# Layer two's memory attention first, sample steps per pair of heads, six state updates after the gates: a two-layer hybrid decoder step on one Trainium2 core

## The chip, the core and the metric

The kernel runs on one core of a Trainium2 chip. The metric is device time in microseconds: the median of the runs, and beside it one profiled execution with the busy times of the engines. PE is TensorE (its matmuls; PEld are its weight loads), DVE is VectorE, ACT is ScalarE, POOL is GpSimd, and SP issues the large transfers. A projection is a product of a 2048 x 128 block of weights with the activations of 264 tokens.

## What is computed

One step of a trunk of two layers for 256 prompt tokens and 8 sample tokens that share the weights. Layer one is sliding-window attention. Layer two, where the change lies, is an HGRN2 recurrence with 12 heads. Both have four memory cross-attention heads, a SiLU gate, an output projection and a LayerNorm. For layer two the reference says, shortened:

```
q, f, iv, mq, g = _split(h @ w_in, HG_SPLITS)
fg = lb + (1 - lb) * sigmoid(f);  qh = silu(q);  kh = 1 - fg;  gh = log(fg)
# per token t, head h:  state = fg * state + kh (x) v ;  o = qh . state
o = o * rsqrt(mean(o*o) + eps) * norm_w                  # per head
mem_o = softmax(mq . mk / sqrt(128)) . mv                # 4 memory heads
branch = concat(o, mem_o) * silu(g);  y = branch @ w_out
h = LN(alpha * h + y)
```

For the prompt the recurrence starts from zero and runs in chunks; its last state is an output. For each of the 8 samples the 12 states (128 x 128 numbers each) are read, used for one token, updated and written back, and the memory keys and values come from a cache.

## The kernel before

**The stream.** All weights and caches come as units of 128 x 2048 f32 numbers (1 MB), in an order written out in the code (`stream.add`). `Stream.load` (L79) has SP fetch a unit into one of four raw slots. `Stream.prep` splits it into two f16 halves: ACT writes the high half (L97), DVE the low half (L98). At most four units are split ahead. `Stream.run` then calls the unit's function. A projection (`proj`) is 16 blocks with three matmuls each (high x high, high x low, low x high, L303 to L305). A raw slot is free for the next load once its unit is split, except for a state unit, whose raw numbers are updated in place and written out.

**Side work.** After each unit, `after` calls `pump(1)`, which runs one step of the generator at the head of the queue `side`: a pair's chunked recurrence (`hg_side`, ten steps) or one memory head's prompt attention (`memp_side`, two steps). The lists `later` and `due` put off short pieces by one unit.

**The planner.** The code gives a program order, dependences and a few fixed orders (`issue_after`, `keep_in_program_order`). A planner sets the order of each engine's instructions and gives out the slots of the tile pools when the program is built, from priorities that follow the program order and from its own estimates of durations.

**Layer two.** Heads go in pairs. Per pair come two forget-gate units (`f_unit`), two value units (`hv_unit`), and per head a query unit (`hq_unit`), a state unit of half size (`state_unit`) and, for heads 0 to 7 (`NG1`), that head's gate (`early_gate`, stored unmultiplied in `mix`). The query unit of the odd head appends the pair's `hg_side`. A state unit forms the sample token's output: eight samples, each one matmul of two columns and one of one column against the state's halves (L1222, L1223), two all-ones matmuls for q.k (L1226), and small DVE and ACT operations on 8 numbers per partition (L1212 to L1229). Then it updates the state: eight selection matmuls spread the value rows (`vb`, L1233), ACT scales the state by the forget gate (L1237), DVE adds k times v (L1238), and POOL stores it to `ss_o` (L1241). `f_unit` makes `ks8`, the scaled k, for this (L1003).

After the sixth pair come the four memory queries (`mq_unit`); the last of them appends the four `memp_side`. Then four units of cached keys (`ck_unit`, small matmuls into `mss`; after the fourth a softmax with two transposes back, `mback`, L677), and four of cached values (`cv_unit`, `mso`), with the gates 8 to 15 (`gate_unit`) between and behind them. A gate from 8 on is multiplied in by `gate_fin` once its head is done.

The output projection has 16 units (`out_unit`). The last eight are done for 176 of the 264 tokens first and keep their halves (`hold`, a pool that opens when layer two's pool has been closed); the other 88 tokens follow while the first 176 are normalised.

Of the kernel before, what the change touches and what calls it, by code (L numbers as in the profile page):

```python
# [18 lines left out]
P = 128  # L19
NC = 16  # L20
# [13 lines left out]
NG1 = 8  # L34
# [12 lines left out]
LEVELS = (1, 2, 4, 8, 16, 32, 64)  # L47
NMASK = (len(LEVELS) - 1) * 64

# [8 lines left out]
class Stream:  # L58


    def __init__(self, nc, pool, nraw, nsplit):
        self.nc, self.pool = nc, pool
        self.nraw, self.nsplit = nraw, nsplit
        self.units = []
        self.raw = {}
        self.hl = {}

# [37 lines left out]
    def run(self, pump):  # L105
# [11 lines left out]
        for i in range(n):  # L117
# [8 lines left out]
            while free < prepped and (free <= i or self.units[free][5]):  # L126
                free += 1
# [7 lines left out]
def trunk_kernel(  # L135
# [75 lines left out]
    bias_s = pm.tile([P, 2, NQ], F32, name="bias_s")  # L211

# [770 lines left out]
    def f_unit(h):  # L983
        def fn(hl):
# [6 lines left out]
            if i == 0:  # L991
# [3 lines left out]
                cur["ks8"] = p1.tile([P, 2, TS], F32, tag="ks8", name=f"ks8{h}", bufs=2)  # L995
            fg, kk, ks8 = cur["fg"][:, i], cur["kk"][:, i], cur["ks8"][:, i]
# [6 lines left out]
            nc.vector.tensor_scalar_mul(ks8, kk, 1.0 / (SA * SK))  # L1003
# [5 lines left out]
    def hq_unit(h):  # L1009
        def fn(hl):  # L1010
            p1 = H["p"]
            pt = proj(hl, xhl, T, f"hq{h}")
            if h % 2 == 0:
                cur["q"] = p1.tile([P, 2, T], F32, tag="hq", name=f"hqs{h}", bufs=2)
            silu2(cur["q"][:, h % 2], pt)
            if h % 2 == 1:
                side.append(hg_side(h // 2, cur["q"], cur["vn"], cur["fg"], cur["qk"]))
# [3 lines left out]
    later, due = [], []  # L1021

    def hv_unit(h):
        def fn(hl):
# [3 lines left out]
            if i == 0:  # L1028
                cur["vn"] = p1.tile([P, 2, 2, P], F32, tag="vn", name=f"vn{h}", bufs=2)
                cur["vr"] = p1.tile([P, 2, P], F16, tag="vr", name=f"vr{h}", bufs=2)  # L1030
# [10 lines left out]
    def hv_rows(h, vt, vs, vn, vr):  # L1041
# [7 lines left out]
        nc.vector.tensor_copy(vr[:, i], p16)  # L1049
# [14 lines left out]
    def hg_side(pi, q, vn, fg, qk):  # L1064
# [119 lines left out]
        for i, sq in enumerate(sqs):  # L1184
# [3 lines left out]
            scaled = mix[:, h] if h >= NG1 else sq  # L1188
# [3 lines left out]
            if h < NG1:  # L1192
# [4 lines left out]
    def state_unit(h):  # L1197
        def fn(hl):
            p1 = H["p"]
            pi, i = h // 2, h % 2  # L1200
            raw = stream.raw[state_at[h]][:, : TS * P]
            R = raw.rearrange("p (b v) -> p b v", b=TS)
            v = hl[:, :, : TS * P].rearrange("p s (b v) -> p s b v", b=TS)
            vr, fgs, ks8 = cur["vr"][:, i], cur["fg"][:, i, TP:T], cur["ks8"][:, i]
            qs, vts = (cur[n][:, i, TP:T] for n in ("q", "vt"))
            ks = cur["kk"][:, i]
            if i == 0:
                osb[pi] = p1.tile([P, 2, T], F32, tag="osb", name=f"osb{pi}", bufs=2)
            qk = p1.tile([P, TS], F32, tag="qk", name=f"qk{h}", bufs=2)
            qf = p1.tile([P, TS], F32, tag="qf", name=f"qf{h}", bufs=2)  # L1210
            qfh = p1.tile([P, TS, 2], F16, tag="qfh", name=f"qfh{h}", bufs=2)
            nc.vector.scalar_tensor_tensor(qf, qs, SA * 0.5 * CP, fgs, op0=ALU.mult, op1=ALU.mult)  # L1212
            nc.vector.scalar_tensor_tensor(qk, qs, 8.0 * 0.5 * CP / SK, ks, op0=ALU.mult, op1=ALU.mult)
            qkh = p1.tile([P, 2, TS], F16, tag="qkh", name=f"qkh{h}", bufs=2)
            nc.scalar.activation(qkh[:, 0], qk, AF.Copy)
            nc.vector.tensor_tensor(qkh[:, 1], qk, qkh[:, 0], op=ALU.subtract)
            nc.scalar.activation(qfh[:, :, 0], qf, AF.Copy)
            nc.vector.tensor_tensor(qfh[:, :, 1], qf, qfh[:, :, 0], op=ALU.subtract)
            po = bank("ms", 1, f"hos{h}")
            pov = po[:, : 2 * TS].rearrange("p (b s) -> p b s", s=2)  # L1220
            for b in range(TS):
                mm(pov[:, b], v[:, 0, b], qfh[:, b], start=True, stop=False)  # L1222
                mm(pov[:, b, 0:1], v[:, 1, b], qfh[:, b, 0:1], start=False, stop=True)  # L1223
            pq = po[:, 2 * TS : 3 * TS]
            for s in range(2):
                mm(pq, H["ones"], qkh[:, s], start=s == 0, stop=s == 1)  # L1226
            nc.vector.tensor_reduce(qf, pov, axis=AX.X, op=ALU.add)
            nc.vector.tensor_tensor(qk, pq, vts, op=ALU.mult)
            nc.vector.scalar_tensor_tensor(osb[pi][:, i, TP:T], qf, 1.0 / (SA * SA), qk, op0=ALU.mult, op1=ALU.add)  # L1229
            for g in range(2):  # L1230
                pvb = bank("pt", 2, f"vb{h}{g}")
                for bb in range(4):
                    mm(pvb[:, bb * P : (bb + 1) * P], H["sel"][:, 4 * g + bb], vr, start=True, stop=True)  # L1233
                for bb in range(4):
                    b = 4 * g + bb
                    s = R[:, b]
                    nc.scalar.activation(s, s, AF.Copy, scale=fgs[:, b : b + 1])  # L1237
                    nc.vector.scalar_tensor_tensor(  # L1238
                        s, pvb[:, bb * P : (bb + 1) * P], ks8[:, b : b + 1], s, op0=ALU.mult, op1=ALU.add
                    )  # L1240
            nc.gpsimd.dma_start(ss_o[pi, :, i * TS * P : (i + 1) * TS * P], raw)  # L1241
# [3 lines left out]
    state_at = {}  # L1245
    for pi in range(HD // 2):
        for part, unit in (("f", f_unit), ("v", hv_unit)):
            for i in range(2):
                stream.add(wb(w_in1, NB1[part] + 2 * pi + i), unit(2 * pi + i))
        for h in (2 * pi, 2 * pi + 1):  # L1250
            stream.add(wb(w_in1, NB1["q"] + h), hq_unit(h))
            state_at[h] = len(stream.units)
# [180 lines left out]
```

## Time and profile before

| | us |
|---|---|
| median of 3 runs (lowest, highest) | 906.13 (906.07, 907.13) |
| profiled execution | 906.08 |
| its span, first to last instruction | 904.3 |
| PE busy, share of the span | 886.6 (98%) |
| DVE busy | 701.5 (78%) |
| ACT busy | 582.4 (64%) |
| POOL busy | 34.9 (4%) |

Times in the trace count from the first instruction. In this execution layer two's first projection starts at 420 us, the memory queries at 702, the first cache unit at 729 and the output projection at 800. "Idle before" a row is the time in which its engine stood still, and the name behind the arrow is what ended it. Matmuls overlap, so a matmul's own duration is longer than the step from one start to the next; the step is what a matmul costs.

### The profile page before, as it was taken

Reading aid. Unit: us, or ns where it says so; the run is one execution under the profiler, and the core shown is the slowest. Engines: PE = TensorE matmul, PEld = TensorE weight load, DVE = VectorE, ACT = ScalarE, POOL = GpSimd, SP = SyncE. Lnnn points to the kernel's source line nnn. Section 1 sums busy time; section 2 is a strip of 40 time slices with the busy share of each in tenths; the row PEclk is TensorE's granted clock in tenths of the full one; section 3 lists DMA queues with packets and bytes.
Section 4 is the critical chain, followed back from the end, with each engine's and each line's share of the span. In section 5 each row is a group of like instructions: output and inputs, shape, how many; then the busy total and the mean of one; then the engine's idle time right before and its main releaser. Section 6 shows DMA issues by size and latency. Waiting matters only on the chain.

```text
span 904.3 us, 21814 instructions
## 1 busy us (share of the span) xinstructions
PE 886.6 (98%) x9281; PEld 762.9 (84%) x9281; DVE 701.5 (78%) x1230; ACT 582.4 (64%) x982; POOL 34.9 (4%) x68
## 2 busy tenths in 40 slices
PE   9999999999999999999999999999999999799996
PEld 6888889678888888876888888898888888688996
DVE  6879877669886666697687887979788989678736
ACT  6767776657664444476766877777777585858415
POOL 1100010000000000002000000000000000000000
PEclk9999999999999999999999999999999999899999
DMA  9998566557785555556374655827454878456303
GB/s 340 392 353 317 188 245 209 188 208 265 262 333 192 187 192 203 207 198 214 127 292 137 216 201 174 299 101 260 160 215 164 303 283 308 172 207 244 130 2 97
DMA packets 37853, 198.67 MB, mean 220 GB/s; under 512 B 4555, under 2 KB 10732, under 8 KB 17532
## 3 DMA queue, kind: packets, MB, share of 16 engines
q1 hardware_dynamic: 33024, 181.55, 56.3%
q0 software_dynamic: 4688, 15.67, 4.6%
q8 instruction: 72, 1.18, 0.5%
q14 instruction: 25, 0.20, 0.1%
q10 hardware_dynamic: 44, 0.07, 0.0%
HBM read 180.03 MB, written 17.22 MB: 218 GB/s over the span
## 4 chain that ended last, share of the span: by engine, by line
PE 77%; DVE 8%; ACT 6%; DMA 6%; issue 3%; SPq 0%; ACTq 0%; DVEq 0%
PE o L303 5%; PE o L305 5%; PE o L304 5%; PE g L305 5%; PE g L303 5%; PE g L304 5%; DVE hl L98 4%; ACT hl L97 2%; PE hv L305 2%; PE hv L303 2%; PE hv L304 2%; DMA raw<-in_w_in 2%; PE hq L303 2%; PE hq L305 2%; PE hq L304 2%
## 5 line engine op out<-in xcount | busy, mean ns | idle before, releaser
L98 DVE SCALAR_TENSOR_TENSOR hl<-raw,hl 128x2048 f16<-128x2048 f32 (+2 forms) x168 | 358.6, 2138 | 82.0 <-ACT hl L97 81.0
L97 ACT ACTIVATE hl<-raw 128x2048 f16<-128x2048 f32 (+2 forms) x168 | 299.2, 1784 | 97.8 <-PE o L305 45.4
L305 PEld LDWEIGHTS <-hl 128*128 128x128 f16 (+2 forms) x2048 | 197.4, 98 | 31.8 <-DVE hl L98 2.9
L303 PEld LDWEIGHTS <-hl 128*128 128x128 f16 (+2 forms) x2048 | 197.3, 98 | 30.6 <-issue 2.2
L304 PEld LDWEIGHTS <-hl 128*128 128x128 f16 (+2 forms) x2048 | 197.4, 98 | 30.3 <-issue 2.2
L305 PE MATMUL g<-xhl,hl 128*128 128x264 f16 x512 | 142.0, 277 | 2.4 <-DVE hl L98 2.4
L303 PE MATMUL g<-xhl,hl 128*128 128x264 f16 x512 | 141.9, 277 | 0.0
L304 PE MATMUL g<-xhl,hl 128*128 128x264 f16 x512 | 141.9, 277 | 0.0
L303 PE MATMUL o<-mix,hl 128*128 128x264 f16 x384 | 105.4, 276 | 0.8 <-DVE xres L747 0.8
L304 PE MATMUL o<-mix,hl 128*128 128x264 f16 x384 | 105.8, 276 | 0.0
L305 PE MATMUL o<-mix,hl 128*128 128x264 f16 x384 | 105.7, 276 | 0.0
L303 PE MATMUL q<-xhl,hl 128*128 128x264 f16 x192 | 53.0, 276 | 1.0 <-DVE kst L251 1.0
L303 PE MATMUL f<-xhl,hl 128*128 128x264 f16 x192 | 52.9, 276 | 0.4 <-DVE mvhl L251 0.4
L305 PE MATMUL hv<-xhl,hl 128*128 128x264 f16 x192 | 53.0, 276 | 0.0
L303 PE MATMUL hq<-xhl,hl 128*128 128x264 f16 x192 | 53.0, 276 | 0.0
L304 PE MATMUL hq<-xhl,hl 128*128 128x264 f16 x192 | 53.0, 276 | 0.0
L305 PE MATMUL hq<-xhl,hl 128*128 128x264 f16 x192 | 53.0, 276 | 0.0
L304 PE MATMUL hv<-xhl,hl 128*128 128x264 f16 x192 | 53.0, 276 | 0.0
L303 PE MATMUL hv<-xhl,hl 128*128 128x264 f16 x192 | 53.0, 276 | 0.0
L304 PE MATMUL q<-xhl,hl 128*128 128x264 f16 x192 | 53.0, 276 | 0.0
L305 PE MATMUL q<-xhl,hl 128*128 128x264 f16 x192 | 53.0, 276 | 0.0
L304 PE MATMUL f<-xhl,hl 128*128 128x264 f16 x192 | 52.9, 276 | 0.0
(338 smaller groups left out, 1858.4 us busy)
## 6 DMA issues: line engine op xcount, KB each, us to landing
raw<-in_w_in SPq DMA_DIRECT2D x88, 1024.0 KB, 6.4
raw<-in_w_o SPq DMA_DIRECT2D x32, 1024.0 KB, 5.0
raw<-in_w_mk SPq DMA_DIRECT2D x8, 1024.0 KB, 4.9
raw<-in_w_mv SPq DMA_DIRECT2D x8, 1024.0 KB, 4.9
raw<-in_c_mk SPq DMA_DIRECT2D x8, 1024.0 KB, 5.1
raw<-in_c_mv SPq DMA_DIRECT2D x8, 1024.0 KB, 7.0
raw<-in_state SPq DMA_DIRECT2D x12, 512.0 KB, 5.4
out_ss<-raw POOLq DMA_DIRECT2D x12, 512.0 KB, 5.5
```

The source lines that it names most:

```text
L97: hi = self.nc.scalar.activation(hl[:, 0, s], raw[:, s], AF.Copy, scale=scale)
L98: lo = self.nc.vector.scalar_tensor_tensor(hl[:, 1, s], raw[:, s], scale, hl[:, 0, s], op0=ALU.mult, op1=ALU.subtract)
L303: mm(out, lhs(0), rhs(0), start=start, stop=False)
L304: mm(out, lhs(0), rhs(1), start=False, stop=False)
L305: return mm(out, lhs(1), rhs(0), start=False, stop=stop)
```

## The change

Layer two's units get another order, one state unit per pair takes the place of two, and six heads' state updates move into the output projection.

- **Order.** `f 0`, the four memory queries, the four key-cache and four value-cache units stand among the units of pairs 0 and 1; state units are dealt out by hand. `EARLY` gates are those of heads 0, 1, 2 and 6; the other twelve gates follow the last pair, with 10 and 11 last.
- **Pumps.** `pumps` says for each unit how many side steps run after it (0, 1 or 2 in place of 1).
- **State per pair.** One 1 MB unit for two heads: the small operations work on 16 numbers, the all-ones matmuls on 16 columns, so there are 12 in place of 24. `sel` carries the scale that `ks8` had. For pairs 0 to 2 head `2 pi` is updated at once and the other one unit later (`later`), and `stream.longer` keeps the raw slot one unit longer in the program order.
- **Put off.** For heads 6 to 11 (`LATER`) the forget gates and keys are copied behind the value rows and stored to DRAM (`kept`). At the seventh of the twelve gates POOL fetches `sel`, the kept rows and the first three states again, the states into the memory heads' tiles `mkhl`, `mvhl` and `mqhl`, which are free by then. Output units 1, 3, 5, 7, 9 and 11 each update one head and fetch the state that is three further on into the home just used.

```
-NG1 = 8
+EARLY = (0, 1, 2, 6)
+LATER = tuple(range(6, HD))
...
-            while free < prepped and (free <= i or self.units[free][5]):
+            while free < prepped and (free + self.longer.get(free, 0) <= i or self.units[free][5]):
...
-            nc.vector.tensor_scalar_mul(ks8, kk, 1.0 / (SA * SK))
...
-                cur["vr"] = p1.tile([P, 2, P], F16, tag="vr", name=f"vr{h}", bufs=2)
+                cur["vr"] = p1.tile([P, 2, KEPT], F32, tag="vr", name=f"vr{h}", bufs=2)
...
+    def update(h, R, vr, fgs, ks, sel):
+        for g in range(2):
+            pvb = bank("pt", 2, f"vb{h}{g}")
+            for bb in range(4):
+                mm(pvb[:, bb * P : (bb + 1) * P], sel[:, 4 * g + bb], vr, start=True, stop=True)
+            for bb in range(4):
+                b = 4 * g + bb
+                s = R[:, b]
+                nc.scalar.activation(s, s, AF.Copy, scale=fgs[:, b : b + 1])
+                nc.vector.scalar_tensor_tensor(
+                    s, pvb[:, bb * P : (bb + 1) * P], ks[:, b : b + 1], s, op0=ALU.mult, op1=ALU.add
+                )
+        nc.gpsimd.dma_start(ss_o[h // 2, :, h % 2 * TS * P : (h % 2 + 1) * TS * P], R.rearrange("p b v -> p (b v)"))
+
+    def fetch(h):
+        if not homes:
+            aside["sel"] = cp.tile([P, TS, P], F16, tag="ms", name="late_sel", bufs=2)
+            nc.gpsimd.dma_start(aside["sel"], sel_d)
+            aside["kept"] = cp.tile([P, len(LATER), KEPT], F32, tag="ms", name="late_kept", bufs=2)
+            for pi in sorted(kept):
+                k = 2 * pi - LATER[0]
+                nc.gpsimd.dma_start(aside["kept"][:, k : k + 2], kept[pi])
+            for t in (mkhl, mvhl, mqhl):
...
+        homes.rotate(-1)
+        aside[h] = homes[-1]
+        nc.gpsimd.dma_start(aside[h], state[h // 2][:, (h % 2) * TS * P : (h % 2 + 1) * TS * P])
...
+    def with_update(fn, k):
+        def f(hl):
+            fn(hl)
+            late_update(LATER[k])
+            if k + 3 < len(LATER):
+                fetch(LATER[k + 3])
...
+            split_from(qfh[:, :, :, 0], qfh[:, :, :, 1], qf, 1.0)
+            split_from(qkh[:, 0], qkh[:, 1], qk, 1.0)
...
+                mm(pq, H["ones"], qkh[:, s].rearrange("p i b -> p (i b)"), start=s == 0, stop=s == 1)
...
+            if 2 * pi in LATER:
+                tail = vr[:, :, P // 2 :]
+                nc.vector.tensor_copy(tail[:, :, :TS], fgs)
+                nc.vector.tensor_copy(tail[:, :, TS:], ks)
+                nc.gpsimd.dma_start(kept[pi], vr)
+                return
...
+            half(0)
+            later.append(lambda: half(1))
...
+    f_of(0)
+    for h in range(NM):
+        w1("mq", h, mem1_sides(mq_unit(h)) if h == NM - 1 else mq_unit(h))
+    cache(c_mk, ck_unit, 0)
+    f_of(1, 2)
+    cache(c_mk, ck_unit, 1)
+    v_of(0, 2)
+    cache(c_mk, ck_unit, 2)
+    v_of(1)
+    cache(c_mk, ck_unit, 3)
+    q_of(0)
+    gate_of(0)
+    cache(c_mv, cv_unit, 0)
+    gate_of(1)
+    cache(c_mv, cv_unit, 1)
+    q_of(1)
+    cache(c_mv, cv_unit, 2)
+    f_of(2, 2)
+    cache(c_mv, cv_unit, 3)
+    f_of(3, 2)
+    state_of(0)
+    v_of(2, 2)
+    v_of(3, 2)
+    q_of(2)
+    q_of(3)
+    state_of(1)
+    gate_of(2)
+    for pi in range(2, HD // 2):
+        gated = 2 * pi - 2 in EARLY
+        f_of(2 * pi, 2)
+        f_of(2 * pi + 1, 2)
+        v_of(2 * pi, 2)
+        v_of(2 * pi + 1, 1 if gated else 2)
+        q_of(2 * pi)
+        q_of(2 * pi + 1)
+        state_of(pi)
+        if 2 * pi in EARLY:
+            gate_of(2 * pi)
...
+    for k, j in enumerate([j for j in range(NC) if j not in EARLY and j not in last] + list(last)):
+        w1("g", j, fetch_first(gate_unit(1, j)) if k == 6 else gate_unit(1, j))
     for i in range(NC):
-        stream.add(wb(w_o[1], i), out_unit(1, i), home=hold if i >= NC - NSPLIT else None)
+        unit = out_unit(1, i)
+        if i % 2 == 1 and i // 2 < len(LATER):
+            unit = with_update(unit, i // 2)
+        stream.add(wb(w_o[1], i), unit, home=hold if i >= NC - NSPLIT else None)
...
-        pump(1)
+        pump(pumps.get(i, 1))
...
-        sel[b, b] = 1
-        sel[TS + b, b] = 1
+        sel[b, b] = 1 / (SA * SK)
+        sel[TS + b, b] = 1 / (SA * SK)
```

139 lines of the change are left out of this document (70 added, 69 removed).

## The prediction

> **What bounds the kernel now.** I read the page first, then who waited for whom on PE, then the busy times by stretch, then single rows where PE stood still.
>
> ```profile
> span 904.3 us, 21814 instructions
> ...
> PE 886.6 (98%) x9281; PEld 762.9 (84%) x9281; DVE 701.5 (78%) x1230; ACT 582.4 (64%) x982; POOL 34.9 (4%) x68
> ...
> PEclk9999999999999999999999999999999999899999
> ```
>
> PE is busy in 886.6 of 904.3 us, so an edit pays by matmuls it takes out or by moments in which PE stands still or runs at a lower clock. The granted clock dips in one slice, the 35th of 40, near 780 us. The waits of PE, layer two up to 736 us (first row) and 736 to 806 us (the rest), say the same:
>
> ```profile
> PE f L303 <- DVE mvhl L251: 0.4, 1, 0.4
> ...
> PE g L305 <- DVE hl L98: 2.4, 2, 1.7
> PE hpo L1169 <- ACT st L1147: 1.5, 1, 1.5
> PE mback L677 <- DVE mrows L674: 1.0, 1, 1.0
> PE msc L303 <- ACT osq L1183: 0.4, 1, 0.4
> PE hpo L1171 <- ACT s L1162: 0.3, 1, 0.3
> ```
>
> In 317 us of recurrences PE waits 0.4 us; in the 70 us behind them, where the memory attention, the last two recurrences and the late gates meet, 2.4 + 1.5 + 1.0 + 0.4 + 0.3 = **5.6 us**. The stretches (span, then busy time of PE, PEld, DVE, ACT, POOL, then granted clock, DMA share, GB/s) show why:
>
> ```profile
> 419.00:455.00 36.00, 35.57 (x334) 30.75 (x332) 21.46 (x46) 25.27 (x49) 6.16 (x11) 1.00 0.49 171
> ...
> 508.00:561.00 53.00, 52.85 (x565) 46.71 (x564) 45.12 (x89) 39.02 (x70) 2.14 (x4) 1.00 0.61 211
> ...
> 736.00:765.00 29.00, 28.37 (x363) 24.94 (x361) 28.97 (x33) 19.94 (x21) 0.00 (x0) 1.00 0.89 328
> 765.00:785.00 20.00, 15.56 (x231) 12.93 (x229) 12.74 (x22) 13.88 (x22) 0.54 (x1) 0.91 0.45 165
> ...
> 806.00:848.00 42.00, 41.23 (x371) 35.63 (x370) 33.73 (x37) 28.73 (x28) 0.00 (x0) 1.00 0.60 223
> 848.00:876.00 28.00, 28.00 (x372) 28.00 (x370) 11.10 (x27) 2.87 (x8) 0.00 (x0) 1.00 0.01 2
> ```
>
> The first stretch (heads 0 and 1 before any recurrence runs) leaves DVE 14.5 of 36 us free. A full pair, 508 to 561, has DVE 45.1 in 53 (85%) and PE does not wait. From 736 to 765 DVE is busy in 28.97 of 29 us: there a PE-cheap cache unit follows nearly every gate. Then the split weights run out and PE loses 4.4 of 20 us. These rows show how cheap a cache unit is for PE:
>
> ```profile
> 777.00 0.17 PE L696 MATMUL mso<-msphl,hl 128*128 128x2 f16 x1
> ...
> 777.25 0.16 PE L696 MATMUL mso<-msphl,hl 128*128 128x2 f16 x1
> ...
> 788.78 0.28 PE L304 MATMUL g<-xhl,hl 128*128 128x264 f16 x1
> ...
> 789.68 0.28 PE L303 MATMUL g<-xhl,hl 128*128 128x264 f16 x1
> ```
>
> Ten steps in 0.25 us make 25 ns, and 32 of them 0.8 us a cache unit; eight steps in 0.90 us make 112.5 ns, and 48 of them 5.4 us a projection. DVE and ACT split the same megabyte for either:
>
> ```profile
> L98 DVE SCALAR_TENSOR_TENSOR hl<-raw,hl 128x2048 f16<-128x2048 f32 x69 | 158.0, 2292 | 23.9 <-ACT hl L97 23.4
> L1238 DVE SCALAR_TENSOR_TENSOR raw<-vb,ks,raw 128x128 f32<-128x128 f32 x96 | 26.7, 345 | 0.2 <-PE vb L1233 0.2
> L98 DVE SCALAR_TENSOR_TENSOR hl<-raw,hl 128x1024 f16<-128x1024 f32 x12 | 14.7, 1222 | 1.8 <-ACT hl L97 1.7
> L734 DVE SCALAR_TENSOR_TENSOR sil<-sil,g 128x264 f32<-128x264 f32 x8 | 3.4, 428 | 0.0
> ...
> L1237 ACT ACTIVATE raw<-raw,fg 128x128 f32<-128x128 f32 x96 | 29.5, 391 | 3.5 <-DVE hl L98 3.5
> L1226 PE MATMUL hos<-qkh,ones 128*128 128x8 f16 x24 | 2.3, 166 | 0.0
> ```
>
> **The change, part by part.** *Removed from the end of layer two:* the eight cache units, the four memory queries and the memory heads' prompt work. Twelve gates remain there with the last recurrence: PE 12 x 5.4 = 64.8, and about 7.5 of the 9.8 us that the pair row leaves beside its eight projections (53 - 43.2), 72 us in all. DVE: 12 splits, 27.5; the pair's own work, 45.1 less its splits (8 x 2.29 + 2 x 1.22 = 20.8) and updates (16 of 96, 4.5), 19.8, which includes two gates; three operations of 0.43 for each of the other ten, 12.9. That is 60 of 72 us, 84%, the share of the pair row, under which PE did not wait. So I cost the old cluster as gone. Its price is more than the idle 5.6:
>
> ```profile
> 762.55 0.28 PE L304 MATMUL g<-xhl,hl 128*128 128x264 f16 x1
> 763.46 0.29 PE L305 MATMUL g<-xhl,hl 128*128 128x264 f16 x1 [0.63 <-DVE hl L98]
> ...
> 785.63 0.43 PE L303 MATMUL g<-xhl,hl 128*128 128x264 f16 x1
> 785.85 0.43 PE L304 MATMUL g<-xhl,hl 128*128 128x264 f16 x1
> ...
> 776.00:780.00 4.00, 3.63 (x53) 2.88 (x53) 0.23 (x1) 3.94 (x7) 0.00 (x0) 0.77 0.50 207
> 780.00:784.00 4.00, 3.71 (x95) 3.10 (x93) 3.67 (x8) 4.00 (x5) 0.00 (x0) 0.81 0.01 4
> 784.00:788.00 4.00, 2.56 (x12) 1.79 (x13) 4.00 (x5) 4.00 (x8) 0.00 (x0) 0.62 0.32 100
> ```
>
> A wait of 0.63 lengthened the step to 0.91 us where 0.11 is usual, so each costs 0.17 beside its idle time: 6 x 0.17 = **1.0**. Behind the cluster the step is 0.22 in place of 0.11 at a granted clock near a half. In 784 to 788, a clock of 0.62 means 0.38 x 4 = 1.5 us lost; in 776 to 784, 0.23 x 4 + 0.19 x 4 = 1.7 at most, of which PE used part: I take 0.8. Sum **8.9**, bounds 5.6 (idle alone) and 5.6 + 1.0 + 3.2 = 9.8.
>
> The Trainium skill, "TensorE: Matmul & The Clock Gate", Part 1, What's actually happening, says that the array's clock falls to a half after at least one idle window of about 3.4 us. By that rule a PE 78% busy (15.56 of 20) would keep its clock and the dip would not go with these short waits, so the gain would be 2.3 smaller, a time of 900.4 (rival D). The rows show the clock halved without any such gap.
>
> *Added in front:* the same units, between pair 0's and 1's projections. From f0 to q0 (nine projections, four cache units) DVE has 13 splits, 29.8, and some 10 us of attention work in some 57 us of PE: it runs ahead. The tight place is **gate 0 to gate 2**: ten projections (54), four cache units (3.2), two state pairs, one full recurrence, a quarter of the next and one memory head give PE about 71. DVE has 16 splits (36.6), the pair's own work 24.3 (45.1 - 20.8), a quarter of the next recurrence (4) and two more heads' updates (4.5): 69.4, or 98%. Bounds for new stalls there: nothing, if the four units split ahead (4 x 2.29 = 9.2 us) cover it, and 8.9 if the old cluster simply comes back. Nearest is 736 to 765, where DVE was full for 29 us and PE lost 0.63 us; scaled to 71 us that is 1.5, with a quarter off since 98% is not full: **+1.2**. The softmax chain behind the last key-cache unit (mback, 1.0 before) now has two projections, 10.8 us, over it; without them it is 1.0 again.
>
> *Sample steps once per pair:* 12 all-ones matmuls of 24 go, 12 x 0.025 = **-0.3** on PE. DVE saves six splits' fixed part (12 x 1.222 - 6 x 2.292 = 0.9) and some 45 operations of about 0.17, ACT about half as much; that lies beside PE and I count it only as margin, zero to 1 us of fewer stalls. The scale folded into the selection matrix costs nothing and takes 12 tiny DVE operations out.
>
> *Six updates put off:* heads 6 to 11 update in the output projection's odd units 1 to 11. One head is 8 of 96: DVE 2.2, ACT 2.5 us; six are 13.4 and 14.8. From 806 to 876 DVE was busy 33.7 + 11.1 = 44.8 and ACT 31.6 of 70, so they become 58.2 and 46.4: hidden behind PE. Without that cover they would cost up to 13.4. PE's selection matmuls are as many as before. POOL issues six more reads of 0.5 MB, three small stores, four small loads and the six stores that it issued before; the updates wait on the reads, and behind a late one on ACT queue the next weights' splits. The first three reads are issued under the gates, over 30 us ahead, the others six output units ahead: zero, at worst 2. On POOL's queue they stand between the stores of states, for which nothing waits but a home's next read.
>
> The Trainium skill, "DMA: Bandwidth & Descriptors", Issuing engines are not separate DMA queues, speaks against this part: transfers issued by POOL share the sixteen DMA engines with the weights, so 3 MB read again and 3 MB stored take their time from the loads. The row of 806 to 848 has the DMA engines at 0.60 and 223 GB/s; 6 MB over 60 us add 100 GB/s, a share of 0.87, and the sum stays as it is unless the loads' lead is already gone (the second rival).
>
> The order of raw buffers is eased: three whole state pairs hold one slot each, where these rows show twelve waits for a store out of a slot:
>
> ```profile
> SPq L79 <- DMA out_ss<-raw: 44.2, 12, 9.1
> ```
>
> The deferred half keeps its slot one unit (5.4) longer; PE felt none of the 44.2, so I count zero, at worst 2.
>
> **Sum.** The profiled run took 906.08, 1.8 above its span; the median of the runs is 906.13, so they agree. 906.1 - 8.9 - 0.3 + 1.2 = **898.1**; I predict **898.0**. Own range 894.5 (all bounds on the good side: 906.1 - 9.8 - 0.3 - 1.0 = 895.0, and some of the 0.8 us elsewhere) to 900.5.
>
> **Rivals.** *A. The early stretch starves.* Place: gate 0 to gate 2. DVE also waits for ACT's high halves (23.4 us in the row of L98), and if it cannot be kept busier than in the pair row, 85%, its 69.4 need 82 against PE's 71; pair 1's recurrence follows at once, so no lead is rebuilt: 11 lost, plus 1.5 for the clock. It decides below 69.4 / 80.2 = 87%. Time 906.1 - 9.2 + 12.5 = **909**. For it: 85% is what the pair stage shows. Against: DVE was not the limit there, and where it was it reached 28.97 of 29.
>
> *B. Part of the gain goes again at the end.* Gates 10 and 11 come last, and output unit 0 needs their rows at its tenth and eleventh of 16 steps; a DVE that is behind, or loads slowed by the second reading, leave 3 to 5 us: **902**. For it: the output stage's DMA share. Against: the gate stage's 84%.
>
> *C. The order is not carried out.* A planner sets each engine's order at build time; if it keeps the cache units near other cheap work, or the cluster only moves, the time is **905.5**. For it: DVE's total work hardly changes. Against: stream order also sets the loads.
>
> *D. The cluster goes, the half clock stays.* The dip of 776 to 788 comes back with any thinner stretch: the term is 6.6 in place of 8.9, **900.4**. For it: the dip lies in 776 to 788, with PE busy in 3.63 and 3.71 of 4 us for most of it. Against: every other slice of layer two has the full clock. [...]
>
> **How the numbers follow.** About 0.2% (1.8 us) is what a measurement of this kernel can tell. Forecast 0.54, D 0.07, B 0.16, C 0.09, A 0.14. Faster: forecast, D, B and a little of C, 0.79; within 0.2%: 0.08; slower: 0.13. The range goes from 894.5 to 906.0: it leaves out A and a little below.
>
> **What would show it.** Right: no row of PE waiting for DVE hl or ACT st in the last gates; clock 1.00 there; L1226 x12; DVE above 93% between gate 0 and gate 2 with PE idle under 2 us. Wrong: PE waits for DVE hl L98 or for a recurrence's products before 560 us (A), PE waits in the first output units for DVE mix or for ACT behind a DMA (B), or the cluster standing at another place with its clock dip (C).

## The result: 2.3% slower, and the profile after

| | before | after |
|---|---|---|
| median of 4 runs (lowest, highest), us | 906.57 (906.07, 907.13) | 926.50 (925.52, 928.66) |
| profiled execution, its span | 906.08, 904.3 | 925.58, 923.8 |
| ratio of medians, 95% interval | | 1.0226 (1.0213 to 1.0239) |

The forecast was 898.0. The page of the kernel after, the same lines that were shown of before:

```profile
span 923.8 us, 21730 instructions
...
PE 892.3 (97%) x9269; PEld 763.8 (83%) x9269; DVE 696.1 (75%) x1176; ACT 579.7 (63%) x964; POOL 41.9 (5%) x81
...
PEclk9999999999999999999999999999999999999999
```

PE, DVE and ACT have about as much to do as before; the 19.5 us are waits of PE and time at a lower clock. The dip in the granted clock near 780 us is gone from the page. Most line numbers are now 3 or 4 higher. The waits of PE (sum, count, longest):

```profile
PE hq L307 <- DVE vs L255: 4.8, 2, 2.9
PE vb L1204 <- DVE mqhl L1209: 2.8, 2, 2.2
PE o L307 <- DVE xres L751: 2.2, 2, 1.6
PE hs L307 <- ACT qk L1082: 1.9, 2, 1.2
...
PE vb L1204 <- ACT vn L1049: 1.6, 1, 1.6
...
PE hd L1123 <- ACT osq L1186: 1.5, 1, 1.5
PE hpo L1172 <- ACT st L1150: 1.2, 1, 1.2
PE rms L1185 <- ACT osq L1180: 1.0, 2, 0.6
```

Of the old rows, gates waiting for DVE hl and `mback` are gone; `hpo` waiting for `st` is still there (1.5 before), and `xres` (0.8 before) belongs to the output projection. The new ones belong to the recurrences (`vs`, `qk`, `vn`, `osq`) and to the updates that were put off (`mqhl`). The stretches show where they lie (span, busy PE, PEld, DVE, ACT, POOL, granted clock, DMA share, GB/s):

```profile
504.00:564.00 60.00, 59.87 (x683) 53.03 (x681) 52.19 (x89) 49.05 (x89) 1.62 (x3) 1.00 0.67 248
600.00:625.00 25.00, 22.42 (x226) 19.70 (x225) 18.40 (x44) 16.12 (x27) 1.61 (x3) 1.00 0.57 212
650.00:676.00 26.00, 21.50 (x182) 17.97 (x179) 10.09 (x22) 15.21 (x35) 1.63 (x3) 0.93 0.38 133
700.00:726.00 26.00, 22.47 (x202) 18.66 (x200) 13.83 (x30) 16.95 (x34) 1.62 (x3) 0.93 0.44 154
736.00:800.00 64.00, 64.00 (x675) 56.42 (x673) 55.02 (x91) 40.23 (x56) 1.62 (x3) 1.00 0.55 191
800.00:826.00 26.00, 21.03 (x202) 17.23 (x200) 17.61 (x41) 11.82 (x20) 3.21 (x6) 0.97 0.52 188
```

The early stretch and the gates (736 to 800) are full. PE loses 2.6, 4.5, 3.5 and 5.0 us around 612, 663, 713 and 820, and the clock of 0.93 takes up to 1.8 more in each of two. In 650 to 676 every engine has room, DVE most of all (10.09 of 26): no engine's load holds PE there; it waits for one step of a recurrence after another.

For comparing kernels I add up, over all matmuls, the step to the next matmul less the median step of that shape before; this holds the waits and the slow clock alike. Lost us by stretch, worked out so from each trace (the last column from the start of the span):

```
                          425-600  600-725  725-800  800-end   all
before                       1.6      1.0     10.3      1.6    22.8
after                        1.5     18.9      0.4     12.2    41.5
updates held (below)         1.5     15.3      1.1      3.7    31.4
pairs only                   1.4      8.6     16.7      4.0    38.7
memory first alone           7.0      3.0      3.1     12.1    33.2
held, two buffers            1.8      1.1      5.3     11.9    29.2
```

The difference of two sums follows the spans to 1 us (after: 18.7 of 19.5). Single rows from 657 us on show how a transition between two pairs goes wrong:

```profile
657.56 1.05 PE L1161 MATMUL pu<-vn,kn 128*128 128x128 f32 x8
658.45 0.38 PE L1048 MATMUL hvp<-ident,hvt 128*128 128x128 f32 x2
...
663.42 0.38 ACT L1037 ACTIVATE hvt<-hv 128x264 f32<-128x264 f32 x1
...
664.27 0.38 PE L307 MATMUL hq<-xhl,hl 128*128 128x264 f16 x1 [2.94 <-DVE vs L255]
...
669.26 2.45 ACT L1208 ACTIVATE mkhl<-mkhl,late_kept 128x128 f32<-128x128 f32 x8 [4.42 <-DMA late_kept<-kept]
```

A pair's value projections leave the matmul banks through `hvt` and `vs`, single buffers that the pair before must have read (`hvp`, `hvr`); in program order those reads stand behind `pu`, a late step of the recurrence. So when the recurrence is late, `pu`, `hvp`, `hvt` and `vs` follow one another, and the next query projection waits for its bank. The last row is a **put-off update at 669 us**, 135 us before the output projection starts. ACT stands idle for 4.42 us ahead of it until a small copy of kept rows has landed, and does 16 scalings; the recurrence's next work for ACT is behind them, and the next recurrence's first product waits for that:

```profile
675.89 1.16 PE L1123 MATMUL hd<-hqs,qk 128*128 128x128 f32 x8 [1.47 <-ACT osq L1186]
```

The chain of recurrences, first and last start of its first product (`hd`) and of its last one (`rms`), before and then after:

```profile
L1120 PE MATMUL hd<-hqs,qk x48: 272/275/275, 459.3 to 731.3; 128*128 128x128 f32 x48
L1182 PE MATMUL rms<-osq,ones_rms x24: 386/386/490, 506.9 to 776.8; 128*128 128x264 f32 x24
```

```profile
L1123 PE MATMUL hd<-hqs,qk x48: 272/275/377, 490.4 to 776.9; 128*128 128x128 f32 x48
L1185 PE MATMUL rms<-osq,ones_rms x24: 386/386/490, 558.3 to 817.7; 128*128 128x264 f32 x24
```

Before, the six follow one another in (731.3 - 459.3) / 5 = 54 us on average (52 to 53 between the first five, 61 from the fifth to the last), and the last ended 23 us ahead of the output projection (799.9). After, the first starts 31 us later, the last ends 41 us later, and that is 13 us behind the output projection's first matmul (804.3). In between the delay is larger still: the first recurrence takes 69 us from `hd` to `rms` where it took 48, so the second starts 52 us later than before (563.9 against 511.9).

### The profile page after: what moved, and what is told of

Its sections match the earlier page's. It is cut to its first block, busy times and chain, and to the rows that moved or that the text cites. A ratio compares the mean times of both kernels' runs of the same rounds, so it can differ in the third digit from the quotient of the medians.

```text
span 923.8 us, 21730 instructions
## 1 busy us (share of the span) xinstructions
PE 892.3 (97%) x9269; PEld 763.8 (83%) x9269; DVE 696.1 (75%) x1176; ACT 579.7 (63%) x964; POOL 41.9 (5%) x81
## 4 chain that ended last, share of the span: by engine, by line
PE 63%; issue 20%; ACT 6%; DMA 6%; DVE 5%; POOL 1%; SPq 0%; ACTq 0%; POOLq 0%; DVEq 0%
PE g L307 6%; PE g L308 6%; PE g L309 6%; PE o L307 4%; PE o L308 4%; PE o L309 4%; ACT hl L100 2%; DVE hl L101 2%; PE mq L308 2%; PE mq L309 2%; PE mq L307 2%; PE q L307 2%; PE q L309 2%; PE q L308 2%; PE mk L308 2%
## 5 line engine op out<-in xcount | busy, mean ns | idle before, releaser
L307 PE MATMUL hq<-xhl,hl 128*128 128x264 f16 x192 | 54.5, 284 | 4.9 <-DVE vs L255 4.8
L308 PE MATMUL hq<-xhl,hl 128*128 128x264 f16 x192 | 54.4, 284 | 0.0
L309 PE MATMUL hq<-xhl,hl 128*128 128x264 f16 x192 | 54.3, 283 | 0.0
```

The costliest lines, as they stand in the source:

```text
L307: mm(out, lhs(0), rhs(0), start=start, stop=False)
L308: mm(out, lhs(0), rhs(1), start=False, stop=False)
L309: return mm(out, lhs(1), rhs(0), start=False, stop=stop)
```

## The experiments

Three theories. **C**: the six recurrences are one serial chain; memory work in front of it puts its start back by 31 us, and its slack, the time from its end to the output projection, was 23. **P**: the planner carries the put-off updates out early, in the recurrences' way. **S**: two steps in one go behind the value units block the engines. Each run has the kernel before beside it on the same chip (medians 904.8 to 907.3 us). Unless an interval stands with it, a time is that of one run; the 13 runs of before beside experiments 8 to 10 went from 905.5 to 913.0, so a few us between two single runs tell little by themselves, and the stretches of the traces have to agree.

**1. No update put off.**

```
-LATER = tuple(range(6, HD))
+LATER = ()
```

> All twelve state updates at their pairs, none put off; the rest of the change stays. Theory P (pulled forward): the planner pulls pieces of the put-off updates from the output units into the recurrences (ACT scales at 669 us, behind a DMA for 4.4 us) and in front of output unit 1, and that costs the time. P expects 900 to 910. Theory C (late chain): the six recurrences run one behind another at some 54 us each, their first one starts at 490 us in place of 459, so their end, and with it the output projection, is late whatever else is done. C expects 918 to 928, the first hd at 490 and the last hpo after 805.

Measured 924.3; the last recurrence's output product (`hpo`) at 819 us. Putting off as the kernel does it neither cost nor saved, within single runs. C's numbers came; but a kernel that updates all 12 heads among the recurrences cannot speak against P.

**2. Memory work back behind the last pair.**

```
-    for h in range(NM):
-        w1("mq", h, mem1_sides(mq_unit(h)) if h == NM - 1 else mq_unit(h))
-    cache(c_mk, ck_unit, 0)
-    f_of(1, 2)
+    f_of(1)
...
+    for h in range(NM):
+        w1("mq", h, mem1_sides(mq_unit(h)) if h == NM - 1 else mq_unit(h))
+    tail = deque([(c_mk, ck_unit, t) for t in range(4)] + [(c_mv, cv_unit, t) for t in range(4)])
```

> The memory units go back behind the last pair, among the twelve gates, and the first recurrence's pair comes first; put-off updates (fetched at the twelfth gate), sample steps per pair and two-step pumps stay. C expects the first hd near 455, the last hpo before 785 and 900 to 910. P expects that the updates are still pulled forward: 916 to 926.

Measured 935.1, a miss for both. The chain did start early (464.6) and end early (775.7), but 10.4 us were lost in 600 to 725, the old cluster was back (15.5 in 725 to 800), and 7.6 and 8.4 us were lost ahead of these stretches and behind them. The pairs have four gates less than before as cover for the chain's waits; that this is what cost in 600 to 725 is my reading and not tested.

**3. Pair 0 first, memory work among pair 1.**

```
     f_of(0)
+    f_of(1)
+    v_of(0)
+    v_of(1)
+    q_of(0)
+    q_of(1)
+    for h in range(NM):
+        w1("mq", h, mem1_sides(mq_unit(h)) if h == NM - 1 else mq_unit(h))
+    state_of(0)
```

> Pair 0's six units first, then the memory queries and the cache units among pair 1's; all else as in the changed kernel. C expects the first hd near 458 and the end of the chain some 30 us earlier than the changed kernel's 815, so PE is the bound and the time is 898 to 906. P expects 918 to 927, for the updates are as before.

Measured 924.9. The first recurrence started at 453 us, but the third only at 615, since the memory work now stood between the first three. The last `hpo` came at 814.7, as in the kernel after. By the numbers on record C missed and P's time came; but the lead was not kept, and the updates were as before, so the run separates neither.

**4. Put-off updates held behind the output unit.**

```
-            late_update(LATER[k])
+            with ExitStack() as behind:
+                for ins in (last_mm[0], *steps[2 * k + 1, 0]):
+                    behind.enter_context(tc.issue_after(ins.ins))
+                late_update(LATER[k])
```

> The changed kernel with each put-off update fixed behind its output unit's last matmul, residual sum and square on PE, DVE and ACT, so that the planner cannot pull it forward. P expects all of its loss back: 900 to 906. C expects the stalls between 655 and 690 us to shrink (no ACT behind the DMA) but the last hpo still after 800 and a time of 912 to 920.

Measured **915.4**, 10 us less than after: P's mechanism is shown, for the stretches behind 800 us above all (12.2 lost there became 3.7). As the whole cause it fails: its 900 to 906 did not come, C's 912 to 920 did. Rows of a put-off update in the kernel after, then in this one:

```profile
L1208 ACT ACTIVATE mkhl<-mkhl,late_kept x16: 384/386/402, 669.3 to 828.1; 128x128 f32<-128x128 f32 x16
...
L1204 PE MATMUL vb<-late_kept,late_sel x48: 216/219/229, 814.0 to 852.3; 128*128 128x128 f16 x48
```

```profile
L1209 ACT ACTIVATE mkhl<-mkhl,late_kept x16: 383/386/388, 824.7 to 861.4; 128x128 f32<-128x128 f32 x16
...
L1205 PE MATMUL vb<-late_kept,late_sel x48: 219/219/219, 820.1 to 870.5; 128*128 128x128 f16 x48
```

In the kernel after, 32 of the 48 selection matmuls ran from 814 to 823.5 us, ahead of and among the last recurrence's final steps and in front of the output unit that needed its result; PE waited three times among them for DVE, 2.17 us the longest:

```profile
814.02 0.39 PE L1204 MATMUL vb<-late_kept,late_sel 128*128 128x128 f16 x4
...
823.14 0.38 PE L1204 MATMUL vb<-late_kept,late_sel 128*128 128x128 f16 x4 [2.17 <-DVE mqhl L1209]
...
823.93 0.38 PE L307 MATMUL o<-mix,hl 128*128 128x264 f16 x2 [0.41 <-ACT mix L733]
```

The 15.3 us lost in 600 to 725 stayed.

**5. The same with the last steps of a recurrence one per unit.**

```
-        v_of(2 * pi, 2)
-        v_of(2 * pi + 1, 1 if gated else 2)
+        v_of(2 * pi, 1 if gated else 2)
+        v_of(2 * pi + 1)
         q_of(2 * pi)
-        q_of(2 * pi + 1)
+        q_of(2 * pi + 1, 2)
```

> The kernel with the updates held behind the output projection (915.4 us in the run before), and within each pair the same number of recurrence steps dealt otherwise: the last three steps of a recurrence (state product, output product, its square and sum) go one per unit, the two-step units stand earlier or behind the second query. Theory S (two latency-bound steps run in one go behind the value units make the stalls at 610, 660 and 708 us): those stalls, 15 us together, fall below 8, time 905 to 910. Theory C (the six recurrences are a chain of about 53 us each that no dealing shortens): stalls only move, last output product still behind 800 us, time 912 to 919.

Measured 915.5, and 17.1 us lost in 600 to 725: the same. S falls, at least for this dealing.

**6. Held, with the memory work spread over pairs 1 to 5 and its steps in a queue of their own.**

```
+    filled = {
+        0: [lambda: gate_of(0), lambda: gate_of(1)],
+        1: [lambda: gate_of(2), lambda: mq_of(0)],
+        2: [lambda: mq_of(1), lambda: mq_of(2)],
+        3: [lambda: mq_of(3)],
+        4: [lambda: gate_of(8)],
+        5: [],
+    }
+    parts = {4: (c_mk, ck_unit), 5: (c_mv, cv_unit)}
...
         pump(pumps.get(i, 1))
+        mem_step()
```

> Updates held as before; pair 0 stands first, the four memory queries and eight cache units stand among pairs 1 to 5 so that 53 us of projections lie between the starts of two recurrences, the memory steps have a queue of their own and no longer stand in line with the recurrences; one step per unit for the last four steps. Theory C (the 31 us by which the memory units put back the first recurrence are what makes the chain last): first recurrence at about 453 us, last output product before 785, time 896 to 903. Rival S alone (bundled steps cost, the start does not): 905 to 910. If both are wrong: 912 or more, with stalls of over 12 us left between 550 and 800.

Measured **905.1**, before beside it 905.5. First recurrence 452.4, last `hpo` 790.5: C's direction, 10 us more regained. The time lies 2 us above C's range and in that of S alone; experiment 5 speaks against S, but this run changes order, dealing and queue together and can't tell them apart. What is left is 6.6 us lost in 600 to 725, where pairs 4 and 5 carry the cache units too, and 5.3 behind 800, with a wait of 2.0 us for the last head's rows.

**7. Sample steps once per pair alone, in the order of before.**

```
-EARLY = (0, 1, 2, 6)
-LATER = tuple(range(6, HD))
+EARLY = tuple(range(8))
+LATER = ()
...
+    for pi in range(HD // 2):
+        f_of(2 * pi)
+        f_of(2 * pi + 1)
+        v_of(2 * pi)
+        v_of(2 * pi + 1)
+        q_of(2 * pi)
+        if 2 * pi in EARLY:
+            gate_of(2 * pi)
+        q_of(2 * pi + 1)
+        state_of(pi)
+        pumps[state_at[pi]] = 2
+        if 2 * pi + 1 in EARLY:
+            gate_of(2 * pi + 1)
```

> The order of the kernel before (pairs with eight early gates, memory units behind them, one step per unit, no update put off), with the sample steps once per pair alone. The prediction costs this part at -0.3 us: 904 to 908. If the larger unit itself (both heads' updates and a state load of twice the size behind one unit) costs: 910 or more, with new stalls between 425 and 700.

Measured **921.7** against 905.5: this part, which I had costed at -0.3, costs 16 us. The stretch at 681 to 690 us in this run:

```profile
681.13 4.78 ACT L1208 ACTIVATE raw<-raw,fg 128x128 f32<-128x128 f32 x16 [1.10 <-DVE hl L101]
...
685.82 0.36 ACT L1165 ACTIVATE s<-pu 128x256 f32<-128x256 f32 x1
686.08 0.36 ACT L1049 ACTIVATE vn<-hvp 128x256 f32<-128x256 f32 x1
...
686.23 0.49 PE L1174 MATMUL hpo<-qk,s 128*128 128x128 f32 x2 [2.02 <-ACT s L1165]
```

Sixteen scalings of the state stand in one block of 4.78 us in ACT's queue, as in nearly every pair of this run. The recurrence's `s` and `vn`, whose inputs are there, come behind them, and PE waits. Before, a pair had two blocks of 8.

**8. The same without the scalings, and 9. with the two heads' updates one and two units later.** The second has, for its edit:

```
-            half(0)
-            later.append(lambda: half(1))
+                with tc.issue_after(last_act[0].ins):
+                    update(2 * pi + i, R[:, i], vr[:, i, : P // 2].bitcast(F16), fgs[:, i], ks[:, i], H["sel"])
...
+            later.append(lambda: half(0))
+            later.append(lambda: later.append(lambda: half(1)))
```

> The order of the kernel before with the sample steps once per pair (921.7 us in the run before), and the ScalarE scaling of the old state left out of every update (96 instructions of 0.3 us; the state outputs are then without the decayed old state). In the run before, 16 such instructions stood in one block of 4.8 us in ScalarE's queue in each pair, ahead of the recurrence's own ScalarE work. Theory U (that block makes the recurrences late): the stall at 684 to 690 us (7.4 us) goes, the last recurrence starts before 737 instead of 748.7, time 903 to 911. Rival L (the larger sample unit is late for another reason: its split of twice the size, its place behind the second query): time 916 or more, last recurrence still starts behind 744.

> The same order with the sample steps once per pair, nothing left out, but the updates of the pair's two heads issued one and two units later, each behind that unit's own ScalarE instruction, so that the block of 16 falls into blocks of about 8. Theory U: 904 to 912, no PE stall above 3 us between 425 and 720 us. Rival L: 916 or more.

Measured 914.4 and 916.4 (before beside them 906.3). Both take away the loss in 600 to 725 (8.6 us became 0.8 and 2.3), so the block is worth 5 to 7 us, and both miss theory U's times; the second lies in rival L's. What stays is the old cluster, 19.4 and 20.0 us in place of 10.3: the last recurrence starts at 741 us, against 730 before. Why the larger sample unit puts it back by 11 us I did not separate further.

**10. Both repairs at once.** The edit is that of 6 with the memory queries behind pairs 0 and 1, the caches among 3 and 5 and only gates 4, 6 and 7 early, and that of 9.

> Both repairs at once: pair 0 first, memory queries among pairs 1 and 2 and cache units among pairs 3 and 5, memory steps in a queue of their own, the last six updates held behind the output projection, and the first six issued one and two units later behind each unit's own ScalarE instruction. Theory C with U: first recurrence at about 453, last one started before 742, last output product before 785; time 897 to 903, so faster than both kernels. If what the earlier run with pair 0 first lost at 692 us and behind 800 us (8.5 us) comes from the load of the vector and scalar engines and not from the order: 904 to 909.

Measured 912.8 (ratio to before 1.0066, 1.0042 to 1.0089). A miss: recurrences 2 and 3 started 66 and 74 us after their predecessors, the last `hpo` came at 804 us, and 9.7 us were lost behind 800.

**11. Before, with memory first alone.**

```
+    w1("f", 0, f_unit(0))
+    for h in range(NM):
+        mq_of(h)
+    cache(c_mk, ck_unit, 0)
...
+    cache(c_mv, cv_unit, 3)
+    q_state(0)
+    q_state(1)
```

> The kernel before with one part of the change alone: the four memory queries, the eight cache units and the eight memory steps stand first (through pair 0), eight early gates, sample steps once per head, one step per unit, nothing put off. Theory C (putting the first recurrence back by some 31 us makes the six-recurrence chain the last thing before the output projection): first recurrence between 485 and 500 us, last output product behind 800, the old stall cluster before the output gone but 8 us or more of stalls behind the last recurrence's start in its place; time 908 to 918. If memory first is good in itself and only the other parts cost: 895 to 901.

Measured 918.7 (two runs, 916.7 and 920.7; ratio 1.0130, 1.0097 to 1.0163), at the upper edge of what was expected of C: **C is shown**. Its chain, and what then bounds the end:

```profile
L1120 PE MATMUL hd<-hqs,qk x48: 272/275/377, 504.1 to 775.2; 128*128 128x128 f32 x48
L1182 PE MATMUL rms<-osq,ones_rms x24: 386/386/490, 561.7 to 814.0; 128*128 128x264 f32 x24
```

```profile
PE o L303 <- ACT mix L729: 4.8, 1, 4.8
```

The recurrences keep their 54 us ((775.2 - 504.1) / 5) and are 45 us later at the start, 37 at the end. The old cluster is gone (3.1 lost in 725 to 800, 10.3 before), and PE waits 4.8 us in one go, up to 819 us, for the last head's rows: its gain went to a wait for the chain (12.1 lost behind 800, 1.6 before). That the chain and not the stream now sets the pace shows in the starts: recurrences two to six each begin 2.5 to 4.3 us behind the last `rms` of the one before, and 5 to 29 us behind the last matmul of their own query projections. Not all of the loss is the chain's: 7.0 us go in 425 to 600, where before lost 1.6, among the cache units, where PE waits 2.3 us for DVE's and ACT's splits and the clock dips (the sign of rival A, which the whole change does not show).

**12. Before, with the memory work in the places of four gates and among pairs 4 and 5.**

```
-NG1 = 8
+NG1 = 4
...
+            if pi in parts:
+                cache(*parts[pi], n)
...
+            elif h < NG1 + NM:
+                mq_of(h - NG1)
```

> The kernel before with the memory work moved without putting back the first recurrence: memory queries in the places of the gates of pairs 2 and 3, cache units among the projections of pairs 4 and 5, memory steps in a queue of their own, those four gates moved to the end (twelve late gates); sample steps once per head, one step per unit, nothing put off. Theory C: first recurrence at 459 us as before, last output product before 790, old stall cluster gone: 897 to 902, faster than both kernels. If a recurrence needs the vector and scalar engines that the cache units' splits take (18 us on the vector engine in pairs 4 and 5): recurrences 4 and 5 are 60 us or more each, last output product behind 795: 903 to 910.

Measured 914.3 (ratio 1.0083, 1.0061 to 1.0104). The first four recurrences start as before (459.0, 511.5, 564.1, 616.9), the next two 76 and 53 us apart, where the cache units stand:

```profile
675.00:745.00 70.00, 59.48 (x678) 49.73 (x676) 54.30 (x113) 49.51 (x87) 2.16 (x4) 0.93 0.57 200
```

PE has 59.5 of 70 us, with DVE at 78% and ACT at 71%: neither is full, PE waits now for a split, now for the recurrence. The second case of the expectation came in part (last `hpo` 797; one of the two steps between starts over 60 us), beyond its price.

**13. Held, with a second buffer for the value projections.**

```
-                cur["vt"] = p1.tile([P, 2, T], F32, tag="vt", name=f"hvt{h}", bufs=1)
+                cur["vt"] = p1.tile([P, 2, T], F32, tag="vt", name=f"hvt{h}", bufs=2)
...
-            vs = H["vs"][i]
+            vs = H["vs"][h % 4]
```

> The kernel with the updates held behind the output projection (915.4 us in its run), with two buffers in place of one for the pair's value projections (and four in place of two for their sample rows; two small buffers of the recurrence made single to find the room). In the traces from pair 2 on, a pair's value projections are taken out of the matmul banks (613, 663, 714 us) only when the pair before has its value rows transposed (608, 659, 711 us), which comes with the last steps of the recurrence before that. Theory B1 (back pressure: this one buffer ties the stream of projections to the chain): the stalls at 613, 663 and 710 us, 15 us together, fall below 6; the chain's end stays behind 795, so that stalls come at the output instead, time 908 to 917. If the buffer is not what ties them: stalls stay at 12 or more, time 914 to 917.

Measured 913.3, 2 us less than without. The stalls between the pairs are gone (15.3 us lost in 600 to 725 became 1.1) and came back at the output (4.8 became 17.2 behind 725), since the chain ends when it did, 806.2 (806.7 without):

```profile
L1186 PE MATMUL rms<-osq,ones_rms x24: 386/386/490, 559.3 to 806.2; 128*128 128x264 f32 x24
```

```profile
PE o L308 <- ACT mix L734: 4.8, 1, 4.8
```

So the single buffer only set where PE waited for the late chain. That it waits is the chain's doing: theory C, in the kernel with the whole change.

**14. Before, and 15. memory first alone, each with two steps per unit.**

```
-        pump(1)
+        pump(2 if side_from <= i < side_to else 1)
```

> The kernel before with two side steps in place of one behind every unit of layer two up to the output projection. It asks what sets the pace of 54 us from one recurrence to the next. Theory U1 (the number of units it is dealt over, with in-order matmuls): the last recurrence starts no earlier than before, since each can start only when its query is projected, but each ends 15 us or more earlier after its start; last rms row before 762; time 903 to 908. Theory L1 (latency of its own scalar and vector work between the splits): recurrences last as long as before (36 to 46 us from hd to hpo), and PE waits more: 908 to 915.

> The kernel with memory first alone (918.7 us in its runs), with two side steps in place of one behind every unit of layer two up to the output projection. Theory U1: the last recurrence still starts at 770 to 775 us but ends 8 us or more earlier (last rms row before 806), time 906 to 912. Theory L1: last rms row at 810 to 816, time 916 to 922.

Measured 927.7 and 917.4 (904.8 beside them). With twice the steps the last `rms` comes at 789.9 in the order of before (776.8 with one step) and at 814.0 with memory first (814.0 with one). Dealing more steps does not make the chain end earlier; theory U1 falls. The numbers of L1 came for 15; the price of 14 lies beyond L1's: recurrences and memory steps now crowd together, and 18.1 us are lost in 725 to 800.

No version was faster than the kernel before; the nearest, experiment 6, is equal to it within what one run can tell.

## Why the prediction was wrong, step by step

- **The old cluster gone, 8.9 us: right.** The loss in 725 to 800 went from 10.3 to 0.4. (The reading that the last two recurrences stood there before was wrong: the fifth had ended at 729 us, and only the sixth did.) The clock dip went with it from this place, so rival D's 900.4 falls. The half clock came back with the new stalls (0.93 in two stretches, 0.97 in a third), which is the sign named for rival C, and also what D says of thinner stretches.
- **Twelve all-ones matmuls, -0.3: right in count.** The row shows 12 of them; each still takes a step of 25 ns, as the 24 did:

```profile
L1271 PE MATMUL hos<-qkh,ones 128*128 128x16 f16 x12 | 1.2, 169 | 0.0
```

- **The tight place, +1.2: it cost nothing** (1.5 lost in 425 to 600, 1.6 before). DVE was busy in 52.6 of 63.5 us from gate 0 to gate 2 (478.7 to 542.2), 83%, where the sum had 98%, and in 52.2 of 60 us from 504 to 564, 87%; PE lost 0.13 in each. Rival A falls as a loss of PE. What the sum did not ask is what became of the recurrence there: it is the one that took 69 us in place of 48.
- **"Twelve gates remain there with the last recurrence": the step that failed first.** I weighed busy times of engines in each stretch and had no term for the order in time, so the last recurrence was not where the sum had it: it starts at 776 us, with most of the gates done, and ends at 818, 13 us into the output projection. The chain's end at 777 us and the start of the output projection at 800 were in the trace of before, 23 us of slack. In front of the first recurrence the change puts five more projections (the memory queries and gate 1) and six cache units, 5 x 5.4 + 6 x 0.8 = 31.8 us at the prediction's own prices; 31 were measured. Memory first alone measured +11.4 (918.7 - 907.3) where I forecast about -8.
- **"Sample steps once per pair: -0.3": failed.** Alone it measured +16 (one run). I counted operations and not where they stand: 16 scalings in one block in ACT's queue (5 to 7 us, shown) and a chain that starts its last recurrence 11 us later (seen, its cause open).
- **"Six updates put off: zero, at worst 2": the number came by luck, the mechanism failed.** Against all updates at their pairs (experiment 1, 924.3) the kernel after costs about 1 us. But the updates ran early and not under the output projection; held there they left 915.4, so carrying them out early gave away 10 us. The cover was there. That is the mechanism of rival C (the planner does not carry the order out), in another place than I put it and at a price 21 us off.
- **Raw slots: right.** SP's wait for stored states fell from 44.2 to 24.7 us:

```profile
SPq L82 <- DMA out_ss<-raw: 24.7, 3, 12.0
```

- **Rival B** had its sign, waits in the first output units (12.2 us lost behind 800), but not for its reason: DMA share was 0.52 in 800 to 826. They came from the chain's end and the updates in front of it, as holding the updates shows (3.7 lost).

The parts don't add: +11 (memory first), +16 (per pair) and +10 (early updates) make 37, the whole is +20. The first two delay the same chain: experiment 1 has both, with the gates and the dealing of the change, and costs 17 and not 27. The +10 is counted from the kernel with the updates held, not from before.

**What stays open:** what sets how long a recurrence takes. The steps of 52 to 53 us before are the stream's own: recurrences two to four there start 0.1 to 0.2 us behind the last matmul of their own query projections and 4 to 6 us behind the end of the one before, and PE does not wait. From `hd` to the last `rms` a recurrence took 47 to 49 us in the first four of before. Beside memory work it can take far longer: 69 us (the first of the kernel after), 74 (the fourth of experiment 12). The steps per unit do not explain it (experiments 5, 14, 15); that it is the splits of the cache units on ACT and DVE would fit and is not shown. Alone behind the last pair the last recurrence goes from its first `hd` to its last `hpo` in 44 us before and 37 in experiment 11; which of its small operations wait behind which split in the pairs I did not measure.

## What to carry to other kernels

Before moving work in front of a serial chain, write down the chain's first start, its pace and its slack against the stage that needs its result; here a delay beyond the slack came back as stalls, though every engine had room where PE stalled. An update that is put off in program order is put off only if something holds it there: look for its rows in the trace at the old place. Merging two units of side work also merges their blocks in an in-order queue, so count what waits behind the block, not only the operations saved.

## What was unexpected

That a transfer of a few kept rows, far from any path, could stop ACT for 4.42 us (669.26, shown above) and PE behind it. And in 650 to 676 us the mean granted clock was 0.93 with PE busy in 21.5 of 26 us; its slice from 664 to 668 reads 0.59, at the end of PE's wait of 2.94 us (661.33 to 664.27):

```profile
660.00:664.00 4.00, 1.23 (x11) 0.93 (x10) 3.79 (x12) 4.00 (x8) 1.06 (x2) 0.98 0.26 98
664.00:668.00 4.00, 3.73 (x21) 2.65 (x21) 0.38 (x3) 0.84 (x4) 0.54 (x1) 0.59 0.70 238
668.00:672.00 4.00, 4.00 (x34) 3.38 (x33) 0.00 (x0) 2.74 (x10) 0.00 (x0) 1.00 0.11 45
```

The clock records of the trace put the half clock at 663.87 to 667.28 us, so it began when PE had stood still for 2.54 us; in the window of the same length ahead of it, 660.46 to 663.87, PE was busy for 0.77 us.

The Trainium skill, "TensorE: Matmul & The Clock Gate", Part 1, What's actually happening, asks for an idle window of about 3.4 us; here a lower clock came after a shorter gap than that. In all seventeen traces the granted clock changes only at the ends of windows of 3.41 us. Of the windows at full clock, all 44 in which PE was busy for up to 1.41 us are followed by the half clock (in 31 of them PE did work for a part), 17 of the 83 with 1.42 to 2.65 us, and 1 of 4304 with more. So in these traces the clock goes with the busy share of a window, and PE need not stand still for all of it.
